# Add, residual and RMSNorm on one core: two small first tiles instead of one, and the last tile in smaller pieces scaled in order

## The chip, the cores and the metric

The kernel runs on one core of a Trainium2 chip. The metric is the device time in microseconds (us) of one execution; lower is better. All runs quoted here: one core, granted clock 1.0 in every record, and TensorE is not used. Profiles are of one execution each. "Span" is the time from the first to the last event of that execution; the timed figure is about 1.8 us longer.

## The reference

```python
batch, seq, dim = 32, 2048, 2048            # 65536 rows of 2048 float32
z   = x + residual
rms = sqrt(mean(z ** 2, axis=-1, keepdims=True) + eps)
out = z / rms * gamma                       # gamma has 2048 elements
```

Two inputs of 537 MB are read and one output of 537 MB is written: 1610.6 MB for little arithmetic.

## The kernel before

Each partition holds whole rows. A tile is up to 7 rows on each of 128 partitions (7.3 MB). There are two buffers for z and one area of 11 rows for the residual, in which successive tiles start at row 0 and at row 4, so neighbours share three rows. All loads and stores are issued by SyncE, in program order; its queue is served by 16 DMA engines, each with an equal share of a transfer of 128 partitions.

```python
R, STEP = 7, 4
sizes = [left] + [R] * n_full               # left = 1: a first tile of 1 row, then 73 of 7

def entry(i):                               # where tile i's residual starts in r_area
    if i == 0: return R + STEP - left
    return 0 if i % 2 else STEP

tail = [(0, 3), (3, 5), (5, 7)]             # pieces of the last tile
def parts(i):                               # the three rows shared with the next tile come first
    if i == 0: return [(0, left)]
    return [(STEP, R), (0, STEP)] if i % 2 else [(0, R - STEP), (R - STEP, R)]

def compute(i):
    if i == last:
        before = None
        for a, b in tail:                   # add, square, then scale the piece before
            add(i, a, b); rms = square(i, a, b)
            if before is not None: scale(i, *before)
            before = (a, b, rms)
        scale(i, *before); return
    done = []
    for a, b in parts(i):
        add(i, a, b)                                  # VectorE, frees residual rows
        done.append((a, b, square(i, a, b)))          # ScalarE, one row at a time
    for d in done: scale(i, *d)                       # VectorE, one row at a time
# ... load_r, load_x, store, add, square, scale: one transfer or one engine's loop each ...

load_x(0); load_r(0); load_gamma(); load_r(1)
compute(0); store(0)
load_x(1); load_x(2)
compute(1); load_r(2)
for i in range(2, n_tiles):
    store(i - 1)
    compute(i)
    if i + 1 < n_tiles:
        load_r(i + 1)       # waits until the shared rows have been added
        load_x(i + 1)       # waits until store(i - 1) has landed
store(last)
```

## Time and profile before

| | before |
|---|---|
| time, median of 3 runs | 3731.92 us (3730.58 to 3732.2) |
| span of the profiled run | 3728.7 us |
| VectorE (DVE) busy | 62% |
| ScalarE (ACT) busy | 29% |
| HBM traffic over the span | 432 GB/s |

The page's slice view, before: the span in 40 slices, the DMA engines' busy share in tenths and the GB/s of each slice.

```profile
DMA  9999999999999999999999999999999999999999
GB/s 408 423 433 433 434 433 434 433 434 435 433 433 433 433 433 434 434 434 434 434 433 435 434 434 433 433 433 433 433 434 434 434 435 434 434 434 434 433 433 403
```

The DMA engines are busy everywhere and move 433 to 435 GB/s in all slices but the first two and the last. So whatever can be saved is at the two ends, and it is small. The Trainium skill ("DMA: Bandwidth & Descriptors", section "Where 436 GB/s comes from") derives a ceiling of 435.2 GB/s for the 16 ports through which the DMA engines reach SBUF; the middle of this trace runs at 434.

One end is the start. Fine windows, before (start:end, length, busy time and instruction count of VectorE, ScalarE and GpSimd, clock, DMA share, GB/s), and the timeline's lines of SyncE's issues in that stretch (start, duration, engine, line, what):

```profile
75.00:78.00 3.00, 3.00 (x2) 0.00 (x0) 0.00 (x0) 1.00 0.75 325
78.00:81.00 3.00, 2.51 (x2) 0.00 (x0) 0.00 (x0) 1.00 0.05 19
81.00:84.00 3.00, 2.56 (x1) 0.00 (x0) 0.00 (x0) 1.00 1.43 612
```

```profile
54.10 0.33 SPq L82 DMA_DIRECT2D r_area<-in_residual_dram  x1
80.54 0.34 SPq L90 DMA_DIRECT2D out_dram<-z  x1
```

(A view counts a packet's whole time and bytes in the window in which the packet starts. So short windows scatter, and a share can exceed 1.)

The load issued at 54.10 us was the last that could be queued. It ended near 78.6 us on the first of the 16 engines and at 81.36 us on the last, and the next transfer, the store of tile 1, was issued only at 80.54 us, when tile 1 had been scaled. In between most DMA engines stood still.

The other end is the tail. Fine windows of before:

```profile
3700.00:3705.00 5.00, 3.41 (x3) 4.94 (x6) 0.00 (x0) 1.00 0.82 356
3705.00:3710.00 5.00, 5.00 (x3) 0.78 (x3) 0.00 (x0) 1.00 0.40 172
3710.00:3715.00 5.00, 4.96 (x4) 0.00 (x0) 0.00 (x0) 1.00 1.02 433
```

From 3700 to 3710 us the DMA share is 0.82 and then 0.40. That looks like 4 us lost. The timeline of VectorE tells why: the store of the first three rows can be issued only after their scaling.

```profile
3699.46 0.17 DVE L116 RECIPROCAL rstd<-rms 128x3 f32<-128x3 f32 x1
3701.59 0.17 DVE L116 RECIPROCAL rstd<-rms 128x2 f32<-128x2 f32 x1 [1.96 <-ACT rms L108]
3701.67 11.36 DVE L119 SCALAR_TENSOR_TENSOR z<-z,rstd,gamma_tile 128x2048 f32<-128x2048 f32 x5
```

The scaling of the first piece (from 3701.67 us) stands behind the reciprocal of the second piece, which waited 1.96 us for ScalarE.

Two more readings need the single records behind these views. The trace has a record for each DMA packet: a 57344-byte packet (7 rows of one partition) takes 2116 ns at the median. And it has a record for each semaphore increment of a DMA: a full transfer makes 16 of them, one for each DMA engine. Below, "landings" are these 16 moments; their first and last tell how far the slowest engine is behind the fastest. The records do not say which engine a packet or a landing belongs to. Numbers of both kinds are worked out from those records, not copied from a view.

### The profile page before, as it was taken

What the parts mean: (1) busy time and instruction counts of PE and PEld (TensorE: products, weight loads), DVE (VectorE), ACT (ScalarE), POOL (GpSimd) and SP (SyncE); (2) the same over time, 40 slices, a digit from 0 to 9 for tenths busy, and PEclk for the clock granted to TensorE, in tenths of its full rate; (3) what the DMA queues carried; (4) which work ended last, traced back from release to release, by engine and by line L of the source; (5) the groups of instructions that cost most, each with busy time, mean ns of one, the idle gap of its engine ahead of it and who ended that gap; (6) DMA issues with size and microseconds to landing.
All of it is one profiled execution on the core that took longest, in us unless ns stands there. A gap on an engine that the chain in (4) does not pass through costs nothing.

```text
span 3728.7 us, 2557 instructions
## 1 busy us (share of the span) xinstructions
DVE 2301.9 (62%) x812; ACT 1071.7 (29%) x1174; POOL 0.2 (0%) x4
## 2 busy tenths in 40 slices
DVE  5566555566565566565566565566665566665566
ACT  2233322333322333322233322233322233322233
POOL 0000000000000000000000000000000000000000
DMA  9999999999999999999999999999999999999999
GB/s 408 423 433 433 434 433 434 433 434 435 433 433 433 433 433 434 434 434 434 434 433 435 434 434 433 433 433 433 433 434 434 434 435 434 434 434 434 433 433 403
DMA packets 32572, 1610.82 MB, mean 432 GB/s; under 512 B 3620, under 2 KB 3620, under 8 KB 3620
## 3 DMA queue, kind: packets, MB, share of 16 engines
q1 hardware_dynamic: 32544, 1610.63, 99.9%
q14 instruction: 20, 0.16, 0.0%
q10 hardware_dynamic: 8, 0.03, 0.0%
HBM read 1073.77 MB, written 536.87 MB: 432 GB/s over the span
## 4 chain that ended last, share of the span: by engine, by line
DMA 67%; DVE 24%; ACT 8%; issue 0%; DVEq 0%; ACTq 0%; SPq 0%
DMA z<-in_x_dram 33%; DMA out_dram<-z 33%; DVE z L95 15%; DVE z L119 9%; ACT sq_junk L101 8%; DMA r_area<-in_residual_dram 1%; DMA r_area<-in_gamma_dram 0%; ACT rms L108 0%; DVE rstd L116 0%; DVE gamma_tile L155 0%; DVEq L204 0%; DVE r_area L150 0%; ACTq L152 0%; DVEq L95 0%; SPq L90 0%
## 5 line engine op out<-in xcount | busy, mean ns | idle before, releaser
L95 DVE TENSOR_TENSOR z<-z,r_area 128x6144 f32<-128x6144 f32 (+3 forms) x148 | 1109.0, 7535 | 1293.7 <-DMA z<-in_x_dram 1287.1
L101 ACT ACTIVATE sq_junk<-z 128x2048 f32<-128x2048 f32 x512 | 963.4, 1882 | 2624.9 <-DVE z L95 2613.5
L119 DVE SCALAR_TENSOR_TENSOR z<-z,rstd,gamma_tile 128x2048 f32<-128x2048 f32 x512 | 1169.4, 2343 | 5.2
L101 ACT ACTIVATION_READ_ACCUMULATOR sq_junk<-z 128x1 f32 x512 | 95.4, 186 | 0.0
L116 DVE RECIPROCAL rstd<-rms 128x3 f32<-128x3 f32 (+3 forms) x148 | 25.6, 173 | 111.1 <-ACT rms L108 111.1
L108 ACT ACTIVATE rms<-ssq,eps_tile 128x3 f32<-128x3 f32 (+3 forms) x148 | 43.9, 297 | 4.8
L155 DVE LOAD_MASK_SELECT gamma_tile<-r_area x1 | 0.0, 14 | 4.7 <-DMA r_area<-in_gamma_dram 4.7
L101 ACT ACT_TABLE_LOAD x1 | 1.3, 1283 | 4.4 <-issue 4.4
L155 DVE STREAM_SHUFFLE gamma_tile<-r_area 128x2048 f32<-128x2048 f32 x1 | 2.3, 2294 | 0.0
L150 DVE MEMSET r_area<- 128x2048 f32 x1 | 1.8, 1765 | 0.4 <-issue 0.4
L108 ACT ACT_TABLE_LOAD x1 | 1.3, 1283 | 0.0
L65 DVE MEMSET eps_tile<- 128x1 f32 x1 | 0.1, 59 | 0.8 <-PEq L190 0.8
L190 POOL MEMSET const-bfloat16-1.0<- 128x1 bf16 x1 | 0.1, 101 | 0.0
L190 POOL MEMSET const-uint8-127<- 128x1 uint8 x1 | 0.1, 101 | 0.0
L190 POOL MEMSET const-float32-0.0<- 128x1 f32 x1 | 0.1, 98 | 0.2 <-issue 0.2
L190 POOL MEMSET const-float32-1.0<- 128x1 f32 x1 | 0.1, 98 | 0.0
## 6 DMA issues: line engine op xcount, KB each, us to landing
r_area<-in_residual_dram SPq DMA_DIRECT2D x73, 7168.0 KB, 27.2
z<-in_x_dram SPq DMA_DIRECT2D x72, 7168.0 KB, 33.8
out_dram<-z SPq DMA_DIRECT2D x72, 7168.0 KB, 34.6
z<-in_x_dram SPq DMA_DIRECT2D x2, 2048.0 KB, 28.7
out_dram<-z SPq DMA_DIRECT2D x2, 2048.0 KB, 9.9
z<-in_x_dram SPq DMA_DIRECT2D x1, 3072.0 KB, 24.2
out_dram<-z SPq DMA_DIRECT2D x1, 3072.0 KB
z<-in_x_dram SPq DMA_DIRECT2D x1, 1024.0 KB, 4.8
```

The lines of the kernel that those rows point to most:

```text
L65: nc.vector.memset(eps_tile, float(eps))
L95: nc.vector.tensor_add(out=z, in0=z, in1=r_area[:, o + a : o + b, :])
L101: nc.scalar.activation(out=sq_junk, in_=z_slots[i % 2][:, a + g, :], func=Act.Square, accum_out=ssq[:, g : g + 1],)
L108: nc.scalar.activation(out=rms[:, :n], in_=ssq[:, :n], func=Act.Sqrt, bias=eps_tile, scale=inv_d)
L116: nc.vector.reciprocal(out=rstd[:, :n], in_=rms[:, :n])
L119: nc.vector.scalar_tensor_tensor(out=row, in0=row, scalar=rstd[:, g : g + 1], in1=gamma_tile, op0=mult, op1=mult,)
L150: nc.vector.memset(stage, 0.0)
L155: nc.vector.stream_shuffle(gamma_tile, stage, [0] * 32)
L190: nc = _bacc.Bacc("TRN2", target_bir_lowering=False, num_devices=1)
```

## The change

Its intent is to close both holes. Two first tiles of 3 and 5 rows let all four first loads be issued at once (16.8 MB), which covers the time until the first stores; and a last tile in pieces of 2, 2, 2 and 1 rows makes the first of its stores ready sooner. A one-buffer tile for the tail's reciprocals forces each piece to be scaled before the next reciprocal.

```diff
-    sizes = [left] + [R] * n_full
+    lead = [3, 5]
+    assert left + R == sum(lead)
+    sizes = lead + [R] * (n_full - 1)
@@
-    tail = [(0, 3), (3, 5), (5, 7)]
+    tail = [(0, 2), (2, 4), (4, 6), (6, 7)]
@@ parts
-            return [(0, left)]
-        return [(STEP, R), (0, STEP)] if i % 2 else ...
+            return [(0, 2), (2, sizes[0])]
+        return [(STEP, sizes[i]), (0, STEP)] if i % 2 else ...
@@ scale
+        if i == last:
+            rstd = stats.tile([P, 4], fp32, name="rstd_tail", bufs=1)
+        else:
+            rstd = stats.tile([P, 4], fp32, name="rstd")
@@
     load_r(1)
+    load_x(1)
     compute(0)
-    store(0)
-    load_x(1)
-    load_x(2)
-    compute(1)
-    load_r(2)
-    for i in range(2, n_tiles):
+    for i in range(1, n_tiles):
         store(i - 1)
         compute(i)
```

(Cut: `entry` and the row that stages gamma follow the new sizes.)

More of the change, by code (lines that the diff above doesn't have):

```diff
@@ L40 @@
     left = (n_rows - n_full * P * R) // P
-    assert n_full * P * R + left * P == n_rows and 0 < left <= STEP
-    sizes = [left] + [R] * n_full
+    assert n_full * P * R + left * P == n_rows
+    lead = [3, 5]
+    assert left + R == sum(lead)
+    sizes = lead + [R] * (n_full - 1)
     starts = [0]
@@ L68, in entry @@
         if i == 0:
-            return R + STEP - left
+            return R + STEP - sizes[0]
         return 0 if i % 2 else STEP
-    tail = [(0, 3), (3, 5), (5, 7)]
+    tail = [(0, 2), (2, 4), (4, 6), (6, 7)]
     def parts(i):
         if i == 0:
-            return [(0, left)]
-        return [(STEP, R), (0, STEP)] if i % 2 else [(0, R - STEP), (R - STEP, R)]
+            return [(0, 2), (2, sizes[0])]
+        return [(STEP, sizes[i]), (0, STEP)] if i % 2 else [(0, R - STEP), (R - STEP, R)]
     def load_r(i):
@@ L114, in scale @@
         n = b - a
-        rstd = stats.tile([P, 4], fp32, name="rstd")
+        if i == last:
+            rstd = stats.tile([P, 4], fp32, name="rstd_tail", bufs=1)
+        else:
+            rstd = stats.tile([P, 4], fp32, name="rstd")
         nc.vector.reciprocal(out=rstd[:, :n], in_=rms[:, :n])
@@ L147, in load_gamma @@
     def load_gamma():
-        row = R + STEP - left - 1
+        row = R
         stage = r_area[:, row, :]
```

## The prediction

> **What bounds the kernel.** The DMA engines. The page's slice view shows DMA at 9 tenths in all 40 slices, and 432 to 437 GB/s from 200 to 3600 us; DVE is busy 62%, ACT 29%. The Trainium skill ("DMA: Bandwidth & Descriptors", Where 436 GB/s comes from) derives a ceiling of 435.2 GB/s; this trace agrees with 434. A two-tile period is 101.5 us, which is 44 MB at that rate. In the DMA packet records a 57344-byte packet takes 2116 ns at the median; summed over one engine's packets that is about 3715 us of the 3728.7 us span. So at most 13 us (0.4%) can be had, at the two ends:
>
> - start: first packet at 1.8 to 2.5 us;
> - a hole at 78 to 81.5 us (fine windows: 19 GB/s in 78 to 81): residual of tile 2 has landed, everything that could be queued is done, and the store of tile 1 is issued only at 80.54 (timeline);
> - three moments (22, 96, 131 us) when one packet on nearly all engines took about 1 us longer;
> - tail: 3704 to 3710 us, DMA share 0.2 to 0.7, because the 3-row store is issued only after its scaling ends, near 3708.7; DVE made both reciprocals first and waited 2.0 us for ACT (timeline);
> - the last landing to the end: 1.4 us.
>
> **What the change does.** Bytes and packet time stay (estimate from the packet durations: 3715.3 us per engine against 3715.1).
>
> Start: four loads are now issued at once, 16.8 MB, which keep the queue busy to about 41 us (estimate at 434 GB/s). Residual 0 lands near 17; adds, squares and scales of 3 rows (2.3 us per row added, 2.0 squared, 2.35 scaled) let store 0 be issued near 35. Residual 2 follows one row's add after x 1 lands, 43 to 46 us, while store 0 runs to 48 us; x 2 near 51; store 1 near 72, with x 2 running to 82. So the hole at 78 us goes: 2.9 us on most engines. The margin before residual 2 is only 1 us.
>
> Tail: the first store can be issued near 3696 instead of 3708.7, the last scaling ends near 3714.6 instead of 3717.8. The share dip at 3704 to 3710 fills. But it is worth almost nothing: a DMA ends on its slowest engine (the skill, same page, Why a DMA increments its semaphore by 16 and not by 1: engines finish independently). The landings of the store before the last tile spread from 3704.5 to 3710.9 us: the slowest engine had no hole, and went straight on with 17 us of stores to 3727.3. What ends earlier are fast engines only. I count 0 to 0.5 us.
>
> The hole at 78 us also did some good: it let an engine that the gamma loads had put 2.6 us behind catch up. Without it that lag stays, and may (I estimate 0.8 us on average) lengthen the slowest engine's run.
>
> Net: -2.9 + 0.8 - 0.2, about -2.
>
> **Prediction.** 3729.9 us, 80% range 3727.0 to 3733.0. Faster by over 2%: 0.005; within 2%: 0.99; slower: 0.005.
>
> **What would show it.** Fine windows: no window under 300 GB/s between 10 and 100 us; DMA share near 1 until about 3712 and then falling as single engines finish; final stores' landings spread over several us instead of under 1 us; steady packets still 2116 ns.
>
> **What would make it wrong.** A hole near 48 us (residual 2 too late); more or fewer of the 1 us moments; a different slowest engine, so that the tail's 4 us do count; packet times altered by the new tile addresses.

## The result, and the profile after

The changed kernel took 3726.53 us at the median of 4 runs (3726.26 to 3728.45), the kernel before 3731.25 us (4 runs). A ratio in this text is the mean time of one kernel's fast runs over that of the other's in the same rounds, so not quite the ratio of the medians. It is 0.9989 here, 95% interval 0.9972 to 1.0007: the same within 2%, as forecast, and too close to 1 to prove a gain from these runs alone. A second set of runs gave 3726.85 us (5 runs) against 3730.87 us (9 runs). The gain is 4 to 5 us by the medians, some 0.12%.

The page's slice view, after:

```profile
DMA  9999999999999999999999999999999999999999
GB/s 419 432 434 434 434 434 434 435 434 434 434 434 434 434 434 434 434 434 434 434 432 434 434 434 434 433 434 434 434 434 434 434 434 434 433 434 434 434 435 397
```

The first two slices rose from 408 and 423 to 419 and 432 GB/s. The last one fell from 403 to 397.

Fine windows of after at the start, and SyncE's issues there:

```profile
75.00:78.00 3.00, 0.00 (x0) 0.00 (x0) 0.00 (x0) 1.00 0.88 382
78.00:81.00 3.00, 0.00 (x0) 0.00 (x0) 0.00 (x0) 1.00 0.88 382
81.00:84.00 3.00, 0.00 (x0) 0.00 (x0) 0.00 (x0) 1.00 1.12 470
```

```profile
47.06 0.33 SPq L84 DMA_DIRECT2D r_area<-in_residual_dram  x1
51.96 0.33 SPq L88 DMA_DIRECT2D z<-in_x_dram  x1
73.50 0.34 SPq L92 DMA_DIRECT2D out_dram<-z  x1
```

The store of tile 1 is now issued at 73.50 us, while loads still run; the hole at 78 us is gone. Fine windows of after at the tail:

```profile
3705.00:3710.00 5.00, 4.86 (x4) 0.00 (x0) 0.00 (x0) 1.00 1.00 426
3710.00:3715.00 5.00, 0.70 (x1) 0.00 (x0) 0.00 (x0) 1.00 0.98 419
3715.00:3720.00 5.00, 0.00 (x0) 0.00 (x0) 0.00 (x0) 1.00 0.57 242
3720.00:3725.00 5.00, 0.00 (x0) 0.00 (x0) 0.00 (x0) 1.00 0.11 46
```

The dip at 3705 to 3710 us is filled, and an equal dip now stands at the very end. The landings tell what that means (us from the span's start):

| | store of the tile before the last: first and last landing | very last landing | from that last landing to the very last |
|---|---|---|---|
| before | 3704.52, 3710.87 | 3727.78 | 16.91 |
| after | 3699.60, 3707.07 | 3724.02 | 16.95 |

The Trainium skill ("DMA: Bandwidth & Descriptors", "Why a DMA increments its semaphore by 16 and not by 1") says that the engines of one transfer finish independently and that only the full count means that all data has landed. This trace agrees: one engine is 6 to 7.5 us behind the fastest by then. The last 7 rows are 16.9 us of work for each engine, estimated from the 2.42 us that a row takes it (2116 ns for 7 rows, times 8 partitions, over 7). From the last landing of the store before it to the very last landing, the table has the same 16.9 us in both kernels, so the engine that was last had no hole in the tail in either.

### The profile page after: what moved, and what is told of

Its sections match the earlier page's. It is cut to its first block, busy times and chain, and to the rows that moved or that the text cites. A ratio compares the mean times of both kernels' runs of the same rounds, so it can differ in the third digit from the quotient of the medians.

```text
span 3724.8 us, 2571 instructions
## 1 busy us (share of the span) xinstructions
DVE 2302.8 (62%) x816; ACT 1072.3 (29%) x1176; POOL 0.2 (0%) x4
## 4 chain that ended last, share of the span: by engine, by line
DMA 67%; DVE 24%; ACT 8%; issue 0%; SPq 0%; DVEq 0%
DMA z<-in_x_dram 34%; DMA out_dram<-z 33%; DVE z L97 15%; DVE z L125 9%; ACT sq_junk L103 8%; ACT rms L110 0%; DVE rstd L122 0%; SPq L84 0%; DVEq L97 0%; SPq L88 0%; DVE rstd_tail L122 0%; DVEq L122 0%
## 5 line engine op out<-in xcount | busy, mean ns | idle before, releaser
L97 DVE TENSOR_TENSOR z<-z,r_area 128x8192 f32<-128x8192 f32 (+2 forms) x150 | 1109.4, 7437 | 1272.7 <-DMA z<-in_x_dram 1270.5
L125 DVE SCALAR_TENSOR_TENSOR z<-z,rstd,gamma_tile 128x2048 f32<-128x2048 f32 x505 | 1153.5, 2344 | 5.2
L122 DVE RECIPROCAL rstd<-rms 128x4 f32<-128x4 f32 (+2 forms) x146 | 25.3, 173 | 117.1 <-ACT rms L110 117.1
L110 ACT ACTIVATE rms<-ssq,eps_tile 128x4 f32<-128x4 f32 (+2 forms) x150 | 44.5, 297 | 4.8
L125 DVE SCALAR_TENSOR_TENSOR z<-z,rstd_tail,gamma_tile 128x2048 f32<-128x2048 f32 x7 | 16.2, 2344 | 0.1
```

Source lines behind the costliest of these rows:

```text
L97: nc.vector.tensor_add(out=z, in0=z, in1=r_area[:, o + a : o + b, :])
L110: nc.scalar.activation(out=rms[:, :n], in_=ssq[:, :n], func=Act.Sqrt, bias=eps_tile, scale=inv_d)
L122: nc.vector.reciprocal(out=rstd[:, :n], in_=rms[:, :n])
L125: nc.vector.scalar_tensor_tensor(out=row, in0=row, scalar=rstd[:, g : g + 1], in1=gamma_tile, op0=mult, op1=mult,)
```

## The experiments

Twelve kernels were run. Times are medians; "before" is the kernel before in the same rounds.

The theories: **A**, the time is that of the slowest DMA engine, so the start made the whole gain and the tail nothing. **B**, the tail's 4 us of idle DMA time made a good part of it. A third question was why the gain was twice my forecast.

### The changed kernel again, and its two halves alone

`e1_start_only` keeps the new start with the old tail, `e2_tail_only` the old start with the new tail.

```diff
# e1_start_only, against the changed kernel
-    tail = [(0, 2), (2, 4), (4, 6), (6, 7)]
+    tail = [(0, 3), (3, 5), (5, 7)]
-        if i == last: rstd = ... "rstd_tail", bufs=1
# e2_tail_only, against the kernel before
-    tail = [(0, 3), (3, 5), (5, 7)]
+    tail = [(0, 2), (2, 4), (4, 6), (6, 7)]
+        if i == last: rstd = ... "rstd_tail", bufs=1
```

> The changed kernel itself once more, for an interval on the size. Main theory (start only counts): 3 to 5 us below the kernel before, and no moment at which packets on nearly all 16 DMA engines take 1 us longer, as the trace of before has at 22, 96 and 131 us. If the vanished moments were chance, this trace may show some, and the gain is then nearer to the 2 us that I predicted.

> The new start with the old tail. Main theory (the time is that of the slowest DMA engine, which had no hole in the old tail): within 1 us of the changed kernel, so 3 to 5 us below before, with the dip of the DMA share in the last 30 us back as in before. Rival (the tail's dip, about 4 us of mean DMA time, is where half or more of the gain came from): 2 to 4 us slower than the changed kernel.

> The old start with the new tail. Main theory: within 1 us of before, although the DMA share no longer dips at 3704 to 3710; the landings of the last store then spread over 5 to 7 us. Rival (the tail pays): 2 to 4 us below before. Also shows whether the hole at 78 to 81 us and the moments of long packets near 22, 96 and 131 us belong to the old start (they come back here) or were chance.

| | median us | runs | before |
|---|---|---|---|
| e0_after | 3726.85 | 3726.45 to 3729.62 | 3730.87 |
| e1_start_only | 3727.18 | 3726.57 to 3727.42 | 3730.87 |
| e2_tail_only | 3730.57 | 3730.33 to 3731.34 | 3730.87 |

The start alone is worth 3.7 us, and its five runs all lie below those of the tail alone, which is worth 0.3 us. Theory B falls. Fine windows of the tail-only kernel show that its tail did what it was made for, with the hole of the old start still there:

```profile
78.00:81.00 3.00, 2.66 (x2) 0.00 (x0) 0.00 (x0) 1.00 0.05 19
3705.00:3710.00 5.00, 4.86 (x4) 2.64 (x6) 0.00 (x0) 1.00 0.95 410
```

In e1_start_only the dip is back:

```profile
3700.00:3705.00 5.00, 5.00 (x3) 2.55 (x5) 0.00 (x0) 1.00 0.35 149
```

And yet the slowest engine took 17.0 us from its landing of the store before the last tile (3707.69 us) to the very last landing (3724.70 us). In e2_tail_only it took 16.9 us.

### A tail bad enough to reach the slowest engine

If A holds, a later first store costs nothing until it is later than the slowest engine, and 1 us for each us from there on. `e5_tail_4_3` cuts the last tile into pieces of 4 and 3 rows; `e4_no_order` keeps the four pieces and drops the one-buffer tile.

```diff
# e5_tail_4_3, against the changed kernel
-    tail = [(0, 2), (2, 4), (4, 6), (6, 7)]
+    tail = [(0, 4), (4, 7)]
# e4_no_order
-        if i == last: rstd = ... "rstd_tail", bufs=1
```

> The changed kernel with the last tile in two pieces of 4 and 3 rows, in order, so that the first store comes about 13 to 15 us later (near 3709 us, first packets near 3710). The slowest engine is then done with the store before it at about 3705.5 and now gets a hole of 4 to 5 us itself, while the fast engines, done near 3699.6, get one of about 10 us. Main theory (only what the slowest engine waits counts): 4 to 5.5 us slower than the changed kernel, so near 3731. Rival (the mean hole of all engines counts): about 9 us slower, near 3736. If the tail did not matter at all: same time.

> The changed kernel without the single-buffer tile that forces the tail's scaling into order; the pieces stay 2, 2, 2, 1. All theories but one: same time as the changed kernel within 1 us, as the last piece is scaled well before the slowest DMA engine reaches its store. Rival (the strict order matters): 2 us or more slower.

Measured: e5_tail_4_3 3730.77 us, e4_no_order 3726.33 us, in the same rounds; before 3732.24 us. The strict order is worth nothing. The late store costs 4.4 us. Fine windows of e5_tail_4_3:

```profile
3700.00:3705.00 5.00, 4.87 (x4) 4.94 (x6) 0.00 (x0) 1.00 0.32 138
3705.00:3710.00 5.00, 4.86 (x4) 1.33 (x3) 0.00 (x0) 1.00 0.00 0
```

Here all engines stood still, the fastest from 3701.06 us, the slowest from 3707.03 us. The slowest took 20.84 us to the very last landing, which is 3.9 us more than 16.9; the mean engine lost about twice as much (7.9 us, by the mean of the 16 landings). The measured 4.4 us is the slowest engine's loss, not the mean one's. With the old tail the first store came just in time for the slowest engine, and that is why smaller pieces brought nothing.

### Is it the small tiles or the order of issue?

`e6_lead_1_7` has the new order of issue with the old sizes.

```diff
-    lead = [3, 5]
+    lead = [left, R]              # 1 row, then 7
```

> The new order of issue (all four first loads at once, nothing issued twice ahead) with the old sizes, a first tile of 1 row and then tiles of 7. Main theory (the hole in the queue, not the number of rows, is what the start costs): the first four loads end at 42 to 44 us, x of tile 2 can only be issued when the small store behind them has landed near 45, so a hole of about 3 us for most engines returns, now near 44 us; it also lines the engines up again. Time within 1.5 us of before, 3729.5 to 3732. Rival (order of issue alone made the gain): like the changed kernel, 3726.5.

Measured: 3732.55 us, 6.2 us over e4_no_order of the same rounds. The hole is back, now at 45 us. Fine windows of e6_lead_1_7:

```profile
42.00:45.00 3.00, 0.00 (x0) 0.00 (x0) 0.00 (x0) 1.00 0.77 325
45.00:48.00 3.00, 2.53 (x1) 0.00 (x0) 0.00 (x0) 1.00 0.06 25
```

The load of x for tile 2 needs the buffer of tile 0, so it could be issued only when the 1-row store, queued behind the four loads, had landed; until then the queue held nothing else. In the changed kernel tile 0's store of 3 rows carries 3 times as much, and it bridges this stretch. So the sizes matter, not the order of issue alone. (The time is a little above my 3729.5 to 3732. In the packet records this hole, from 40 to 60 us, cost 3.8 us per engine, more than the 2.6 of the hole at 78 us in the kernel before.)

### Does the lag of the engine that loads gamma matter?

My forecast had taken off 0.8 us for an engine that the four small gamma loads put behind. `e3_gamma_one` makes them one transfer.

```diff
-        for q in range(4):
-            nc.scalar.dma_start(
-                out=r_area[32 * q : 32 * q + 1, row, :], in_=gamma.partition_broadcast(1))
+        nc.scalar.dma_start(
+            out=r_area[0:128:32, row, :], in_=gamma.partition_broadcast(4))
```

> The changed kernel with gamma loaded by one DMA to 4 partitions instead of four DMAs of one partition each. Main theory: the four loads all ran on one engine and put it about 1 to 2 us behind; spread over four engines the spread of landings of the x load of tile 1 (2.3 us at 44 us) shrinks to about 1 us, and the run is 0 to 1.5 us shorter than the changed kernel. If gamma is not the cause of that lag: spread stays at 2 us and the time is the same.

Measured: 3728.07 us (3726.51 to 3728.89), against 3726.85 us for the changed kernel in the same rounds. The 16 landings of x of tile 1, near 44 us, lay 1.83 us apart instead of 2.19. Some of the lag went, the time did not fall. The reason that I gave for the 0.8 us has no support. But only 0.4 us of the lag went, so this run does not refute it either.

### Long packets

The packet records show a second difference. A 57344-byte packet takes 2116 ns, but some take over 2300, and at some moments nearly every engine has one, which costs about 1 us per engine. The table gives the time above 2116 ns of these packets, as the mean of the 16 engines, in us:

| kernel | 0 to 150 us | 150 to 1800 us | 1800 us to the end |
|---|---|---|---|
| before | 3.04 | 1.11 | 0.24 |
| e2_tail_only (old start) | 2.99 | 1.64 | 0.24 |
| after | 0.33 | 0.46 | 0.32 |
| e0_after (the same kernel) | 1.26 | 0.33 | 1.73 |
| e1_start_only | 2.11 | 0.18 | 0.24 |
| e4_no_order | 1.15 | 0.20 | 0.24 |
| e6_lead_1_7 | 3.30 | 0.47 | 0.41 |

In both kernels with the old start they lie at 22, 96 and 131 us and hit nearly all engines, each time in the last packet before the queue changes between loads and stores. With the new start they lie at 83, 96 and 128 us and hit fewer engines, varying from run to run.

The table flatters the new start, because it has one packet size only. In every kernel nearly all engines have a long packet where the first loads give way to the first store. With the old start that is at 22 us. With the new start it is at 38 to 41 us, in packets of 40960 bytes (x of tile 1), which the table leaves out: 1.0 us per engine in after, 0.8 to 1.1 in the other runs with the new start. The windows of before and of after show it as busy engines that move few bytes:

```profile
21.00:24.00 3.00, 0.00 (x0) 0.00 (x0) 0.00 (x0) 1.00 1.11 325
```

```profile
39.00:42.00 3.00, 0.00 (x0) 0.00 (x0) 0.00 (x0) 1.00 0.94 268
```

So here is the time of all packets of 8192 bytes and more above the usual (median) time of their size, from the start to the store of the tile before the last, per engine; and of that store's 16 landings the last one, with its distance from their mean (all in us):

| kernel | above the usual | last landing | behind the mean |
|---|---|---|---|
| before | 7.7 | 3710.87 | 4.1 |
| e2_tail_only (old start) | 8.0 | 3711.82 | 4.4 |
| after | 5.6 | 3707.07 | 5.0 |
| e0_after (the same kernel) | 7.6 | 3709.82 | 5.5 |
| e1_start_only | 7.1 | 3707.69 | 4.2 |
| e3_gamma_one | 5.5 | 3706.77 | 4.9 |
| e4_no_order | 6.0 | 3706.79 | 4.4 |
| e10_act_long (below) | 6.6 | 3708.25 | 5.1 |

The six profiles with the new start have 6.4 on the mean, the two with the old start 7.8. But single profiles of the new start lie from 0.1 to 2.2 below before: this part of the gain comes and goes from run to run.

A guess at the cause of the long packets: the queue is nearly dry at these moments, because the next residual load waits for an addition. The timeline of before fits this badly at 131 us, for the store that follows there had been issued some 16 us earlier:

```profile
114.47 0.34 SPq L90 DMA_DIRECT2D out_dram<-z  x1
```

### A queue that is never nearly dry

`e11_r_in_two` tests this guess. The residual load of each full tile is split: the 4 rows that no other tile uses are issued right behind the store, before the waiting addition; the 3 shared rows follow as before.

```diff
     for i in range(1, n_tiles):
         store(i - 1)
+        if i + 1 < n_tiles:
+            load_r_part(i + 1, True)      # the 4 free rows
         compute(i)
         if i + 1 < n_tiles:
-            load_r(i + 1)
+            load_r_part(i + 1, False)     # the 3 shared rows
             load_x(i + 1)
```

> The changed kernel with each full tile's residual load cut in two transfers: 4 rows into the part of the area that the tile before does not use, issued right behind a store, and 3 rows where the single load stood. In steady state the single load is issued only 6.7 us after x has landed on the slowest engine, with 17 us of stores queued; when that engine is 7.5 us behind, the fast ones run dry. Traces whose landing spread reached 7.4 us (the changed kernel repeated, the VectorE squares, the tiny instructions) show packets over 2300 ns on most engines from then on, and those runs took about 3 us more. If running nearly dry makes the long packets: 10 us more work is queued here, no long packets in the middle of the run, none near 96 and 128 us either, all runs in the lower group at 3726 to 3727 or up to 1 us below it, and the final spread may pass 8 us. If the long packets have another cause, they stay, and single runs near 3729 stay with them.

Measured: 3730.79 us (5 runs, 3730.68 to 3731.37), before 3730.94. The long packets of 57344 bytes are gone: 0.04 us per engine in the first 150 us, 0.19 and 0.22 in the two later columns. The ones before the first store stay: 0.9 us per engine near 40 us, in packets of 40960 bytes, although the store (issued at 36.64 us) and the next residual load (37.19 us) were queued already. So a longer queue went with fewer long packets at the later moments, but a nearly dry queue is not the whole cause. This is one profile, and the split also changes packet sizes, though the packets of x and of the stores, which were among the long ones, are as large as before. The time, 3730.8 us where I had expected 3726 to 3727, fits the cost of smaller packets, by an estimate. A 32768-byte packet takes 1213 ns and a 24576-byte one 914 ns, 2127 ns together, which is 11 ns more than 2116. At 8 such pairs per engine and tile and some 72 tiles, that is an estimate of 6.3 us; the mean landing of the store of the tile before the last lies 4.8 us later than in after (3706.78 against 3702.01). A split in the first few tiles alone would keep the one and avoid the other; it was not run.

### Instructions on an idle engine

By the middle of a run the engines have drifted apart by several us although each gets the same share. The records show that after each packet of an engine's instruction fetch one 57344-byte packet on one DMA engine takes some 0.2 to 0.5 us longer. `e7_more_act` adds 24 tiny ScalarE instructions to each of 70 tiles, 1680 in all, and `e10_act_long` is its control: more ScalarE time than that, but only 3 instructions per tile, 210 in all.

```diff
# e7_more_act, against the changed kernel
         for d in done: scale(i, *d)
+        if i > 2:
+            for _ in range(24):
+                nc.scalar.activation(out=tiny, in_=rms[:, 0:1], func=Act.Square)     # 128x1
# e10_act_long
+        if i > 2:
+            for _ in range(3):
+                nc.scalar.activation(out=sq_junk, in_=gamma_tile, func=Act.Square,   # 128x2048
+                                     bias=rms[:, 0:1])
```

> The changed kernel with 24 tiny ScalarE instructions (one element per partition) after each of 70 tiles, 1680 in all, in ScalarE's idle time. The traces show 20 instruction-queue packets of 8 KB in 2571 instructions and, right after each, one 57 KB packet that takes 0.25 to 0.48 us longer on one DMA engine. Theory (that is part of why one engine ends 7 us after the fastest): about 13 more such packets, on the engine or two that serve ScalarE, so the final spread of landings grows by 2 to 5 us and the time by 2 to 5 us, with ScalarE still mostly idle. Rival (the spread has other causes, the instruction fetches cost nothing): same time as the changed kernel.

> Control for the run with 1680 tiny ScalarE instructions, which took 9 us more than the changed kernel: the same added ScalarE time (about 5.6 us after each of 70 tiles) in 3 long instructions a tile, 210 in all, whose results nobody uses. If the instruction fetches made the 9 us: one or two more instruction-queue packets (21 or 22 instead of 33) and at most 1 us over the changed kernel. If ScalarE's busy time made them: 9 us again.

Measured: e7_more_act 3735.84 us (4 runs, 3734.91 to 3736.82), 9.5 us over e4_no_order of the same rounds; ratio to before 1.0010. e10_act_long 3727.49 us (5 runs); ratio to before 0.9991, the same as the changed kernel's in its second set. The page's engine line (busy us, share, instructions) and its line of the instruction queue (packets, MB, share) of after, e7_more_act and e10_act_long:

```profile
DVE 2302.8 (62%) x816; ACT 1072.3 (29%) x1176; POOL 0.2 (0%) x4
q14 instruction: 20, 0.16, 0.0%
```

```profile
DVE 2302.8 (62%) x816; ACT 1413.1 (38%) x2856; POOL 0.2 (0%) x4
q14 instruction: 33, 0.27, 0.0%
```

```profile
DVE 2302.7 (62%) x816; ACT 1480.1 (40%) x1386; POOL 0.2 (0%) x4
q14 instruction: 22, 0.18, 0.0%
```

400 us more of ScalarE time in 210 instructions cost nothing that these runs can tell; 340 us in 1680 instructions cost 9.5. That speaks for the number of instructions as what costs, even on an engine that is idle for more than half of the time. (One rival was not tested: the tiny instructions read and write SBUF, the long ones read and write PSUM apart from their bias.) 13 more fetch packets of 8192 bytes for 1680 instructions is one for each 129.

How it costs is only partly as I had expected. The final lag of the slowest engine did not grow (7.29 us, 7.28 without the addition); every engine finished later. In the trace the lag passes 7.2 us at 1931 us and is 8.2 near 2084, and from about 1920 us on most engines have long packets: 6.78 us per engine after 1800 us, against 0.32 in after. A timeline line of e7_more_act at that time, the issue of a residual load:

```profile
2073.90 0.33 SPq L84 DMA_DIRECT2D r_area<-in_residual_dram  x1
```

It could be issued only after an addition of 6.6 us, which in turn had to wait for the slowest engine's landing of x, at 2067.2 us; the fast engines were done with the store before it at about 2076.2 us. Their queue was 2 us from dry. So a lag above some 7 us seems to turn into long packets on all other engines. The other traces agree. The lag of a store's landings first passes 7.2 us at 1830 us in e9_squares_dve, 1931 in e7_more_act, 2388 in e0_after and 2947 in e8_last_row_low8; from 200 us to then these traces have 0.6 to 1.2 long packets per 100 us, and from then on 4 to 12. In the other ten the lag passes 7.2 us only after 3550 us or never, and late long packets are few. It is still a coincidence in time, not isolated by a run.

### Fewer ScalarE instructions

If the fetches make the lag, fewer instructions should shrink it. `e9_squares_dve` moves 2 of 4 squares of each 4-row part from ScalarE to VectorE.

```diff
+            if n == 4 and g >= 2 and 2 <= i < last:
+                nc.vector.scalar_tensor_tensor(out=dve_junk, in0=z_row, scalar=1.0, in1=z_row,
+                                               op0=mult, op1=mult, accum_out=ssq[:, g : g + 1])
+                continue
```

> The changed kernel with two of the seven rows' squares of each full tile moved from ScalarE (two instructions each) to VectorE (one each): some 144 instructions fewer in all, ScalarE's 1176 become about 890, VectorE's 816 about 960. Fetch theory: the busiest instruction stream loses two of its nine 8 KB fetches, worth 0.5 to 1 us on the DMA engine that serves it, so 0 to 1 us faster than the changed kernel; hard to see. VectorE goes from 62% to about 71% busy and stays off the critical path. If it is slower by over 2 us, VectorE delays an issue somewhere.

Measured: 3729.34 us (5 runs, 3729.22 to 3732.08), 1.9 us over e10_act_long in the same rounds. This was a poor test. VectorE went from 816 to 1100 instructions while ScalarE went from 1176 to 892, because the sum costs a second instruction on either engine; the total and the 20 fetch packets stayed. The lag reached 7.3 us by 2000 us in this trace and long packets followed (3.95 us per engine after 1800 us). Why it grew faster is not settled: the same changed kernel reached 6.7 us at 2000 us in one profile and 5.2 in another.

### The last row on eight of the engines

`e8_last_row_low8` cuts the store of the last row into 16 transfers of 8 partitions, to keep the slow engines out of it.

```diff
+            if i == last and b == R:
+                for p in range(0, P, 8):
+                    nc.sync.dma_start(out=rows(o_f, i)[p : p + 8, a:b, :],
+                                      in_=z_slots[i % 2][p : p + 8, a:b, :])
+                continue
```

> A try for a faster version: the last row's store, 1 MB, cut into 16 transfers of 8 partitions. The Trainium skill (DMA: Bandwidth & Descriptors, How many engines) has such a transfer on the 8 lowest-numbered DMA engines only. These then do 4.9 us of it instead of 2.5, the other eight none. If the engine that ends last is one of the upper eight: 2 to 2.5 us faster than the changed kernel (near 3724). If it is one of the lower eight: 2.5 us slower (near 3729). If transfers of 8 partitions spread over all 16 engines: the same time.

Measured: 3733.72 us (5 runs, 3731.16 to 3734.62), before 3730.62; 6.2 us over e10_act_long in the same rounds. Each small store shows 8 landings after the increment that comes with its issue, as eight engines would give; which eight, the records do not say. The timeline of e8_last_row_low8 shows SyncE's 16 issues as one group:

```profile
3714.36 15.44 SPq L94 DMA_DIRECT2D out_dram<-z  x16
```

These 15.44 us are not all time of issuing. By the single records an issue took 0.28 to 1.58 us (0.73 on the mean), and for 3.0 us before the eighth SyncE waited for the landing of an earlier store, with which that issue shares a semaphore. So the last one left only near 3729.8 us, later than the whole of the changed kernel had ended. Whether the placement would have helped was therefore not tested. The Trainium skill ("DMA: Bandwidth & Descriptors", "Issuing engines are not separate DMA queues") calls the time to issue a DMA "usually small relative to the DMA itself"; here the 16 issues add up to 11.6 us, for 1 MB that as one transfer is 2.4 us of work for each engine.

None of the versions tried beats the changed kernel; e4_no_order equals it.

## Why the prediction was right or wrong

- **The bound, and "within 2%": right.** The DMA engines bound both kernels. The slices run at 434 GB/s before and after, and the ratio is 0.9989.
- **The hole at 78 us, -2.9: right.** It cost 2.6 us per engine on the mean (DMA idle time from 70 to 90 us in the packet records, 2.6 before and 0 after), and e1_start_only shows that the start carries the gain. The engine that was last at that time lost little of it (its load landed at 81.36 us), so it had little to win back; that is the lag in the next point but one.
- **The tail, 0 to 0.5 us: right, and for the reason given.** It is worth 0.3 us with the old start (e2_tail_only) and 0.3 with the new one (e0_after against e1_start_only). Both differences lie within the scatter of the runs, so 0.3 is a size, not a proof of more than nothing. e5_tail_4_3 shows the other side: a hole that does reach the slowest engine is paid in full.
- **The lag, +0.8: about the size, its reason not shown.** At the store of the tile before the last the landings lay 6.35 us apart before and 7.47 after; the last one lay 4.1 us behind their mean before and 5.0 after, so the slowest engine gave back 1.0 us (0.1 to 1.5 in the six profiles with the new start). That an early lag stays, as I argued, is doubtful: in e6_lead_1_7 the hole had lined the engines up again (0.8 us apart at 67 us), and they still ended 7.3 us apart.
- **"Bytes and packet time stay", the "three moments" unchanged: this is the term that was mis-sized.** I had listed the three moments as part of the bound and counted 0 for their change, though "more or fewer" of them stood among what would make me wrong. Up to the store of the tile before the last, the packets' time above the usual for their sizes fell from 7.7 to 5.6 us per engine in the profiled run. In the repeat (e0_after) it stayed, at 7.6.

The sum with the measured terms, up to that store: hole -2.6, packet time above the usual -2.1, usual packet time +0.1, lag +1.0, that is -3.6; the last landing moved by -3.8 (3710.87 to 3707.07) and the very last one by the same. I had -2.9 + 0.8 - 0.2, about -2. The missing 2 us are, in this profile, the term that I held at zero. In e0_after, where that term was indeed near zero, the last landing moved by -1.1 only and the run took 3729.36 us, close to my 3729.9. So how far the median lies below my number depends in part on which runs were drawn.

The median of the first set, 3726.53 us, lies 0.5 us below my range (3727.0 to 3733.0), and the repeat, 3726.85, 0.15 below. Taken relative to the kernel before, 0.9989 of 3731.92 is 3727.8 us, inside it. The repeats of the changed kernel fall into two groups, 3726.3 to 3726.9 and 3728.5 to 3729.6. The one profile from the upper group (e0_after) has 3.3 us of long 57344-byte packets per engine, the one from the lower group (after) has 1.1. That fits, but it is one profile each.

Of what I said would show it, three came as written: steady packets of 2116 ns, a share near 1 until about 3715, and final landings spread over 7.3 us. "No window under 300 GB/s between 10 and 100 us" failed by the letter: 39 to 42 us shows 268 GB/s at a DMA share of 0.94, where the loads give way to the first store: the long packets of 40960 bytes, not idle engines. The margin before residual 2 was indeed small, but no hole came at 48 us; the load was issued at 47.06.

What stays open: why packets are long at some changes between loads and stores; why there are fewer of them in some runs of the same kernel; which property makes one engine the slowest, and why its lag grows faster in some runs.

## What to carry to other kernels

In a kernel bound by DMA like this one, the tail is timed by the slowest DMA engine: a dip in the mean DMA share costs nothing while that engine still has work, and everything once it has none, so look at each engine's landings before mending a dip. Queue the next transfer before the queue runs dry: the hole at 78 us cost 2.6 us per engine. Before a packet size or a moment is given the credit for a gain, count all sizes, and look at a second profile of the same kernel. Count instructions even on an engine with time to spare, and before splitting a transfer, compare the summed packet times with the time of the whole.

## What the Trainium skill lacked or had wrong

- "Runtime: NRT & Kernel Launch", "Instruction fetch mechanics": it gives refills in blocks of 16 KiB (256 instructions) and calls their cost "mostly hidden". This trace shows fetch packets of 8192 bytes, one per 129 added instructions, and 1680 tiny ScalarE instructions cost 9.5 us (e7_more_act), where more ScalarE time in 210 instructions cost nothing that the runs can tell (e10_act_long).
- "DMA: Bandwidth & Descriptors": it says that engines finish independently, but not how far apart they get. Here it is 6 to 7.5 us at the end of 3.7 ms with equal shares, and idle DMA time up to that lag was free (e2_tail_only 0.3 us, e5_tail_4_3 4.4 us).
- No page has it that the last packets before a change between loads and stores can be long. Before the first store that cost 0.8 to 1.3 us per engine in all 14 profiles (1.1 in before, 0.9 in e11_r_in_two).
- "DMA: Bandwidth & Descriptors", "Issuing engines are not separate DMA queues": the issue time that it calls "usually small" was 0.28 to 1.58 us for each transfer of 64 KB (e8_last_row_low8).
- "DMA: Bandwidth & Descriptors", "Where 436 GB/s comes from": the ceiling of the ports agrees (434 GB/s in the middle slices). What one packet more costs has to be measured: 2116 ns for 56 KB in one packet, 2127 ns in two.
